# Output projections of a two-layer trunk kernel: tokens loaded two tiles of work ahead, the forms' loads on GpSimd's queue, the last pair of layer 0 in another order

## The chip, the cores and the metric

The kernel runs on one core of one Trainium2 chip. The metric is the device time of one execution in microseconds (us); the time of a kernel is the median of several runs. Engines are called as in the profile: PE is TensorE's matmul, PEld its weight load, DVE is VectorE, ACT ScalarE, POOL GpSimd, SP SyncE. A number such as L256 is line 256 of the kernel before unless the text says otherwise.

## The reference, cut to what matters

One inference step of a trunk with two layers, for 128 prompt tokens and 512 sample tokens (640 together), model width 2048. Everything is fp32.

```python
for layer in range(DEPTH):                       # DEPTH = 2
    hp = rms_norm(xp, norm_g[layer]) * (1.0 + sc_p) + sh_p      # prompt, 128 tokens
    hs = rms_norm(xs, norm_g[layer]) * (1.0 + sc_s) + sh_s      # sample, 512 tokens
    # even layer: banded attention and a gated short convolution
    # odd layer: differential attention and dense attention
    out_p, out_s = mixer(hp, ...), mixer(hs, ...)   # ends in:
    #   return jnp.concatenate([y_a, y_b], axis=-1) @ w_out
    xp = xp + gt_p * out_p                       # gated residual
    xs = xs + gt_s * out_s
```

The change touches the product with `w_out` (2048 x 2048) of both layers, and the `rms_norm` that follows the first layer's residual.

## The kernel before, in words

**Numbers in two parts.** Activations and weights lie transposed in SBUF, 128 channels by 640 tokens to a tile, 16 such tiles (`k` = 0 to 15) for the width. Each fp32 tile is split into a rounded part `hi` (ACT, L220) and the rest `lo` (DVE, L221); a product is three matmuls, weights hi by tokens hi, weights hi by tokens lo, weights lo by tokens hi (L256 to L258 in `proj_q`, L535 to L537 in `run_pairs`). A matmul moves 128 x 320, half of the tokens. A weight block of 512 x 128 is loaded as `raw` on SP's queue (L233) and split in the same way.

**An output projection** (`project_out`, `project`) makes 16 output tiles. The first three go together (`run_tiles`): for each quarter of the width in the order 0, 2, 1, 3 (a *unit*) the four token tiles of that quarter are split and used by the three output tiles, 72 matmuls in all. The fourth tile runs alone. The other 12 go in six pairs (`run_pairs`): seven products Q1, N5, P6, Q2, P7, Q3, P4 of 24 matmuls in place of eight. Four of these take halves of the tokens as they are, three take the *forms* T, sums and differences of halves that `forms` and `make_form` compute from the tiles `j` and `j + 8` (DVE L1083 to L1086 and the split, ACT the rounded part), eight forms in all; the fourth sum `d` goes to `room`, the first 1280 columns of `tables`.

**Where the tokens come from.** The mixers' results `y` are saved to DRAM (`yd`) on GpSimd's queue (L856) and come back twice: as `yin` for the split (SP's queue; layer 0 L865 for tiles 0 to 3 and L1127 for the rest, layer 1 L1586 for tiles 0 to 3 and 8 to 11 and L1127 for the rest) and as `w` for the forms (tag `w8`, four buffers, SP's queue, L1099). A queue takes its issues in the order of the program: a load that waits for a buffer holds back all that stands behind it. In `run_tiles` the four `yin` of a unit are asked for at the unit's start, behind the weights of that unit; L1127 takes the three buffers of `xr`.

**From layer 0 to layer 1.** The last pair's four results make halves of output tiles 14 and 15 (`x1_last`). Half 0 of the tokens is complete with P4's predecessor Q3, half 1 with P4. `norm_half` squares (L1262), sums over the channels with matmuls against ones (L1270: first the sum `acc` of the tiles before, then the last tile's `sq`), takes the power on POOL (L1275), spreads the result with matmuls against `ident` (L1281) and copies it to `sf` (ACT, L1284). Layer 1's first projection then makes its tokens `h` (DVE L1318, L1322, ACT L1320) half by half.

**PSUM.** A projection tile takes a pair of banks (pa, pb) with the number 0, 1 or 2 (`new_pp`; 2 is `Sp`); the three leading tiles take 0, 1, 2 in this order. The gate's result of the last mixer tile is read from its banks by L1003 and L1004.

Of the kernel before, what the change touches and what calls it, by code (L numbers as in the profile page):

```python
# [50 lines left out]
def trunk_kernel(ctx: ExitStack, tc: tile.TileContext, I: dict, O: dict):  # L51
# [195 lines left out]
    last_mm = [None]  # L247

    def proj_q(pp, part, qd, pos, halves=HV, alone=False, js=(0, 4)):
        wh, wl = part  # L250
        for half_i, sl in halves:
            ps = pp[half_i][:, 0:HALF]
            for j in range(*js):
                hi, lo = hs[qd * 4 + j]
                i = j - js[0]
                PE.matmul(ps, wh[:, i, :], hi[:, sl], start=(j == js[0] if alone else (pos == 0 and j == 0)), stop=False)  # L256
                PE.matmul(ps, wh[:, i, :], lo[:, sl], start=False, stop=False)  # L257
                last_mm[0] = PE.matmul(ps, wl[:, i, :], hi[:, sl], start=False,  # L258
                                       stop=(j == js[1] - 1 if alone else (pos == 3 and j == 3)))
# [57 lines left out]
    def run_tiles(jobs, w_ap, make_h, fill=None, rate=0.0, ahead=None, order=(0, 1, 2, 3), before=None,  # L317
                  last=None, by_half=False, mid=False, trans=[], grace=0, cut=None, summed=None, led=None, freed=None):
# [8 lines left out]
        else:  # L327
# [3 lines left out]
               else new_pp(1 + held.index(n) if trans else n) for n in leads}  # L331
# [112 lines left out]
    def run_pairs(cols, w_ap, mov, room, begin, out, tail):  # L444
# [47 lines left out]
        BANK = {"N5": "pb0", "Q3": "pb0", "Q2": "pb1"}  # L492
        seq = [(p, n) for p in range(len(cols)) for n in MOV]
# [32 lines left out]
        for i, (p, name) in enumerate(seq):  # L526
            bank, rows_, new = BANK.get(name, f"pa{(p + 1) % 2}"), mov[MOV[name]], name in ("Q1", "N5", "Q2")
# [22 lines left out]
            if name in ("Q2", "P7") and p == len(cols) - 1:  # L550
                tail(name)
# [306 lines left out]
    def y_maker(tags, width, held=()):  # L858
        def make(k):
            if k in held:  # L860
                drain(attn)
                t = y[k]
            else:
                t = pools["cur"].tile([P, width], F32, tag=tags[k % len(tags)], name="yin", bufs=4 // len(tags))[:, 0:NT]
                nc.sync.dma_start(t, ydram[k])  # L865
            hi, lo = new_h(k)
            split(hi, lo, t)
        return make


# [221 lines left out]
    def forms():  # L1092
# [3 lines left out]
        def load(j):  # L1096
            ts = [big("w8", bufs=4)[:, 0:NT] for _ in range(2)]
            for i in range(2):
                nc.sync.dma_start(ts[i], ydram[j + 8 * i])  # L1099
# [25 lines left out]
    def late_yin(k):  # L1125
        t = pools["cur"].tile([P, NT], F32, tag="xr", name="yin", bufs=3)
        nc.sync.dma_start(t, ydram[k])  # L1127
        split(*new_h(k), t)

# [7 lines left out]
    def project(w, cols, n0, maker, job, begin, out, tail, by_half=False):  # L1137

        go_on = run_tiles([(cols[n], job(n)) for n in range(3)], w, maker, order=(0, 2, 1, 3), by_half=by_half)


# [11 lines left out]
        for n in range(3, n0):  # L1153
            pp, t = new_pp((n - 3) % 2), 4 * (n - 3)
# [14 lines left out]
            if g is not None:  # L1169
# [5 lines left out]
                   "T2": form_of(0), "T3": form_of(1), "T4": form_of(2)}, room, begin, out, tail)  # L1175
        drain(prep)

    def project_out(l, maker, finish, last, tail):
# [35 lines left out]
        project(W_OUT[l], [n * P for n in range(KT)], n0, maker, job, begin, out, tail)  # L1214


    make_y0 = y_maker(("q0h", "q0l", "q1h", "q1l"), NT)
# [4 lines left out]
    def y0_maker(k):  # L1222
        if k < 4:
            return make_y0(k)
        if k == 8:
# [3 lines left out]
            st["acc"], st["sq"] = (mid_tile(n) for n in ("acc", "sq"))  # L1229
            attn.append(forms())  # L1230
        late_yin(k)
# [12 lines left out]
    def x1_last(t, h):  # L1244
        n, sl = KT - 2 + t, HV[h][1]
        if t != h:
            squares(n, sl)
            return
        nc.gpsimd.dma_start(xdram[n], st["xr", n])
        if h:  # L1250
            g = norm_half(n, h)
            advance([g], 1)
            advance([g], 1)
            drain(prep)
# [5 lines left out]
    def norm_half(n, h):  # L1260
        sl = HV[h][1]
        A.activation(st["sq"][:, sl], st["xr", n][:, sl], AF.Square)  # L1262
        yield
# [4 lines left out]
        for i, s in enumerate((st["acc"], st["sq"])):  # L1268
            for b, o in enumerate(starts):
                PE.matmul(tot[:, 4 * i + b:4 * i + b + 1], s[:, o:o + P], ones[:, 0:1], start=True, stop=True)  # L1270
            if i == 0:
                V.tensor_scalar(ss, tot[:, 0:3], 1.0 / D, EPS, ALU.mult, ALU.add)
            else:
                V.scalar_tensor_tensor(out=ss, in0=tot[:, 4:7], scalar=1.0 / D, in1=ss, op0=ALU.mult, op1=ALU.add)
        G.tensor_tensor(r, ss, half[:, 0:3], op=ALU.pow)  # L1275
        for _ in range(1 + h):
            yield
        rt = psT()
        with tc.issue_after(last_mm[0].ins) if h else ExitStack():
            for b, (o, w) in enumerate(((0, P), (P, P), (2 * P, HALF - 2 * P))):  # L1280
                PE.matmul(rt[:, o:o + w], r[:, b:b + 1].to_broadcast([P, P]), ident[:, P - w:P], start=True, stop=True)  # L1281
        if h == 0:
            st["rbc"] = big("sf")[:, 0:NT]
        A.copy(st["rbc"][:, sl], rt[:, 0:HALF])  # L1284
# [3 lines left out]
    def x1_tail(name):  # L1288

        if name == "Q2":  # L1290
            for k in range(4):
                x1_back(k, big("w8", bufs=4))
# [5 lines left out]
    project_out(0, y0_maker, x1_done, x1_last, x1_tail)  # L1298
# [276 lines left out]
    def y1_maker(k):  # L1575
        if k == 4:
# [5 lines left out]
        if k % 8 >= 4:  # L1582
            late_yin(k)
        else:
            t = pools["cur"].tile([P, 768], F32, tag="P", name="yin", bufs=P_BUFS)[:, 0:NT]
            nc.sync.dma_start(t, ydram[k])  # L1586
            split(*new_h(k), t)
# [32 lines left out]
    project_out(1, y1_maker, rows_out, rows_last, lambda name: None)  # L1620
# [49 lines left out]
```

## Time and profile before

| | us |
|---|---|
| median of 3 runs | 2295.93 (2293.33 to 2296.96) |
| the profiled execution, own time | 2294.4 |
| its span in the trace | 2292.6 |
| PE busy | 2255.9 (98%) |
| PEld busy | 2178.0 (95%) |
| DVE busy | 1589.8 (69%) |
| ACT busy | 1088.9 (47%) |
| POOL busy | 160.0 (7%) |

Places in the trace, counted from the span's start: layer 0's output projection begins at 915.5 us (first matmul of its first tile) and its pairs at 976.2; layer 1 begins at 1130.0, and layer 1's output projection at 2072.6.

How to read it: "busy" of PE adds up the modelled durations of pipelined matmuls, so that a PE at 98% can still lose time where no gap is seen; the number of matmuls in a window of fixed length shows it better. In a row of the timeline stand the start, the duration, engine, line, operation, what it writes and reads, and in brackets how long the engine sat idle before it and who released it. "SPq" and "POOLq" are the issues of DMAs by SP and POOL.

### The profile page before, as it was taken

Reading aid. Unit: us, or ns where it says so; the run is one execution under the profiler, and the core shown is the slowest. Engines: PE = TensorE matmul, PEld = TensorE weight load, DVE = VectorE, ACT = ScalarE, POOL = GpSimd, SP = SyncE. Lnnn points to the kernel's source line nnn. Section 1 sums busy time; section 2 is a strip of 40 time slices with the busy share of each in tenths; the row PEclk is TensorE's granted clock in tenths of the full one; section 3 lists DMA queues with packets and bytes.
Section 4 is the critical chain, followed back from the end, with each engine's and each line's share of the span. In section 5 each row is a group of like instructions: output and inputs, shape, how many; then the busy total and the mean of one; then the engine's idle time right before and its main releaser. Section 6 shows DMA issues by size and latency. Waiting matters only on the chain.

```text
span 2292.6 us, 41100 instructions
## 1 busy us (share of the span) xinstructions
PE 2255.9 (98%) x15900; PEld 2178.0 (95%) x15900; DVE 1589.8 (69%) x2831; ACT 1088.9 (47%) x2304; POOL 160.0 (7%) x224
## 2 busy tenths in 40 slices
PE   7999999999999999999999999999999999999999
PEld 5889999999999999999999999999999999999999
DVE  4666968779779776887787665365665655557775
ACT  5325652443522222544464443465565676755443
POOL 1001000000000000000100001011111100000101
PEclk9999999999999999999999999999999999999999
DMA  9985537547367564854553335223223221238642
GB/s 321 294 270 161 158 113 218 152 133 219 116 210 216 177 191 137 277 173 140 164 155 108 116 118 152 79 60 104 79 63 101 71 60 49 76 101 269 184 138 62
DMA packets 380899, 342.89 MB, mean 150 GB/s; under 512 B 16402, under 2 KB 338416, under 8 KB 380192
## 3 DMA queue, kind: packets, MB, share of 16 engines
q1 hardware_dynamic: 366288, 296.00, 43.0%
q0 software_dynamic: 13696, 42.10, 5.4%
q8 instruction: 125, 2.05, 0.4%
q10 hardware_dynamic: 720, 2.16, 0.3%
q14 instruction: 70, 0.57, 0.1%
HBM read 301.27 MB, written 38.93 MB: 148 GB/s over the span
## 4 chain that ended last, share of the span: by engine, by line
PE 85%; DVE 4%; ACT 4%; DMA 3%; issue 3%; POOL 1%; SPq 0%; ACTq 0%; POOLq 0%; DVEq 0%
PE pq L537 7%; PE pq L536 7%; PE pq L535 7%; PE pa L256 6%; PE pa L257 6%; PE pb L256 6%; PE pa L258 6%; PE pb L257 6%; PE pb L258 6%; PE pb L271 2%; PE pb L270 2%; PE pa L270 2%; PE pb L272 2%; PE pa L272 2%; PE pa L271 2%
## 5 line engine op out<-in xcount | busy, mean ns | idle before, releaser
L220 ACT ACTIVATE wh<-raw 128x512 fp32r<-128x512 f32 (+1 forms) x456 | 273.1, 600 | 574.0 <-PE pb L257 406.9
L221 DVE TENSOR_TENSOR wl<-raw,wh 128x512 fp32r<-128x512 f32 (+1 forms) x456 | 295.7, 650 | 212.3 <-ACT wh L220 191.9
L256 PE MATMUL pa<-h,wh 128*128 128x320 f32 x1024 | 325.3, 319 | 4.3 <-ACT h L220 2.0
L257 PE MATMUL pa<-h,wh 128*128 128x320 f32 x1024 | 319.5, 313 | 1.7 <-DVE h L221 0.8
L258 PE MATMUL pa<-h,wl 128*128 128x320 f32 x1024 | 318.2, 311 | 0.9 <-DVE wl L221 0.9
L257 PE MATMUL pb<-h,wh 128*128 128x320 f32 x1024 | 317.1, 310 | 0.0
L258 PE MATMUL pb<-h,wl 128*128 128x320 f32 x1024 | 316.8, 309 | 0.0
L256 PE MATMUL pb<-h,wh 128*128 128x320 f32 x1024 | 316.6, 310 | 0.0
L198 DVE SCALAR_TENSOR_TENSOR acc<-adaw,sT,acc 128x1024 f32<-128x1024 f32 x240 | 299.7, 1276 | 0.0
L256 PEld LDWEIGHTS pa<-h,wh 128*128 128x128 f32 x1024 | 193.1, 189 | 18.3 <-issue 10.0
L257 PEld LDWEIGHTS pa<-h,wh 128*128 128x128 f32 x1024 | 193.3, 189 | 7.6 <-issue 3.3
L535 PE MATMUL pq<-h,wh 128*128 128x320 f32 x640 | 198.7, 311 | 0.4 <-ACT wh L220 0.4
L537 PE MATMUL pq<-h,wl 128*128 128x320 f32 x640 | 198.0, 309 | 0.1
L536 PE MATMUL pq<-h,wh 128*128 128x320 f32 x640 | 197.7, 309 | 0.0
L258 PEld LDWEIGHTS pa<-h,wl 128*128 128x128 f32 x1024 | 193.1, 189 | 3.5 <-issue 2.1
L257 PEld LDWEIGHTS pb<-h,wh 128*128 128x128 f32 x1024 | 192.2, 188 | 1.0 <-issue 0.8
L256 PEld LDWEIGHTS pb<-h,wh 128*128 128x128 f32 x1024 | 192.1, 188 | 0.8 <-issue 0.4
L258 PEld LDWEIGHTS pb<-h,wl 128*128 128x128 f32 x1024 | 192.3, 188 | 0.0
L537 PE MATMUL pq<-T,wl 128*128 128x320 f32 x480 | 147.7, 308 | 0.2 <-DVE wl L221 0.2
L536 PE MATMUL pq<-T,wh 128*128 128x320 f32 x480 | 147.9, 308 | 0.0
L535 PE MATMUL pq<-T,wh 128*128 128x320 f32 x480 | 147.6, 308 | 0.1
L270 PE MATMUL pa<-h,wh 128*128 128x320 f32 x432 | 141.0, 326 | 0.0
(431 smaller groups left out, 5306.0 us busy)
## 6 DMA issues: line engine op xcount, KB each, us to landing
adaw<-in_ada_w SPq DMA_DIRECT2D x128, 512.0 KB, 4.3
raw<-in_ev_w_in SPq DMA_DIRECT2D x176, 256.0 KB, 3.5
raw<-in_od_w_in SPq DMA_DIRECT2D x160, 256.0 KB, 2.9
ada<-in_ada_w SPq DMA_DIRECT2D x32, 1024.0 KB, 7.9
w<-in_od_w_in SPq DMA_DIRECT2D x24, 512.0 KB, 4.0
yd<-y POOLq DMA_DIRECT2D x32, 320.0 KB, 3.2
yin<-yd SPq DMA_DIRECT2D x32, 320.0 KB, 4.5
w<-yd SPq DMA_DIRECT2D x32, 320.0 KB, 4.2
```

Of the source, the lines that this page charges most:

```text
L198: V.scalar_tensor_tensor(out=acc[c], in0=w, scalar=sT[:, kt, c:c + 1], in1=acc[c], op0=ALU.mult, op1=ALU.add)
L220: A.activation(hi, x, AF.Copy)
L221: V.tensor_sub(lo, x, hi)
L256: PE.matmul(ps, wh[:, i, :], hi[:, sl], start=(j == js[0] if alone else (pos == 0 and j == 0)), stop=False)
L257: PE.matmul(ps, wh[:, i, :], lo[:, sl], start=False, stop=False)
L258: last_mm[0] = PE.matmul(ps, wl[:, i, :], hi[:, sl], start=False, stop=(j == js[1] - 1 if alone else (pos == 3 and j == 3)))
L270: PE.matmul(ps, wh[:, j, :], hi[:, sl], start=(qd == 0 and j == 0), stop=False)
L271: PE.matmul(ps, wh[:, j, :], lo[:, sl], start=False, stop=False)
L272: PE.matmul(ps, wl[:, j, :], hi[:, sl], start=False, stop=(qd == 3 and j == 3))
L535: PE.matmul(ps, wh[:, j, :], hi, start=(new and h == 0 and j == 0), stop=False, **kw)
L536: PE.matmul(ps, wh[:, j, :], lo, start=False, stop=False, **kw)
L537: PE.matmul(ps, wl[:, j, :], hi, start=False, stop=(h == 1 and j == 3), **kw)
```

## The change

1. **Loads ahead.** `run_tiles` calls `ahead` for the next unit after the first tile of a unit. The output projections now hand it `y0_ahead` and `y1_ahead`, which issue the next unit's `yin`: in layer 0 tiles 8 and 9 go into the first 1280 columns of `tables`, 10 and 11 and then 4, 5, 6 and 12, 13, 14 into `xr`; 7 and 15 are still loaded at their split. In layer 1, 8 to 11 go to the buffers `P`, the rest to `xr`. The pool "even" is closed, and "mid" opened, at the call rather than at the split of tile 8.
2. **Forms' loads** are issued by GpSimd instead of SP.
3. **Banks** change places in layer 1's output projection (`flip`): the leading tiles take 1, 2, 0, and the pairs' banks are exchanged.
4. **The last pair of layer 0** runs Q1, N5, P6, P7, Q3, Q2, P4; its `xd` loads of layer 1's first tiles are issued at P7 and Q2 (two each) instead of all at Q2.
5. **The two norm halves** at the end of layer 0 are issued elsewhere. Half 1's matmuls are bound to follow particular matmuls of layer 1's first unit (`last_mm` holds four of them).

```diff
-                last_mm[0] = PE.matmul(ps, wl[:, i, :], hi[:, sl], start=False,
+                last_mm[j % 4] = PE.matmul(ps, wl[:, i, :], hi[:, sl], start=False,
...
-               else new_pp(1 + held.index(n) if trans else n) for n in leads}
+               else new_pp(1 + held.index(n) if trans else banks[n]) for n in leads}
...
-        BANK = {"N5": "pb0", "Q3": "pb0", "Q2": "pb1"}
-        seq = [(p, n) for p in range(len(cols)) for n in MOV]
+        LATE = ("Q1", "N5", "P6", "P7", "Q3", "Q2", "P4")
+        BANK = {"N5": f"pb{flip}", "Q3": f"pb{flip}", "Q2": f"pb{1 - flip}"}
+        seq = [(p, n) for p in range(len(cols)) for n in (LATE if late and p == len(cols) - 1 else MOV)]
...
             for i in range(2):
-                nc.sync.dma_start(ts[i], ydram[j + 8 * i])
+                nc.gpsimd.dma_start(ts[i], ydram[j + 8 * i])
...
+        go_on = run_tiles([(cols[n], job(n)) for n in range(3)], w, maker, order=(0, 2, 1, 3), by_half=by_half,
+                          ahead=ahead, banks=(1, 2, 0) if flip else (0, 1, 2))
...
+    def y0_ahead(qd, js):
+        if qd == 2:
             close("even")
             open_pool("mid")
             lay_out("T7 T6 T5 T4 sf xr w8 sx")
             st["acc"], st["sq"] = (mid_tile(n) for n in ("acc", "sq"))
+            for k in (8, 9):
+                yin_at(k, tables[:, (k - 8) * NT:(k - 7) * NT])
+        for k in range(4 * qd + (2 if qd == 2 else 0), 4 * qd + (4 if qd == 2 else 3)):
+            yin_load(k, "xr", 3)
+
+    def y0_maker(k):
+        yin_split(k, *(("q0h", "q0l", "q1h", "q1l")[k], 1) if k < 4 else ("xr", 3))
+        if k == 8:
             attn.append(forms())
...
     def norm_half(n, h):
         sl = HV[h][1]
         A.activation(st["sq"][:, sl], st["xr", n][:, sl], AF.Square)
-        yield
+        for _ in range(1 + h):
+            yield
+
+        def behind(j):
+            es = ExitStack()
+            if h:
+                es.enter_context(tc.high_priority())
+                es.enter_context(tc.issue_after(last_mm[j].ins))
+            return es
...
-        for _ in range(1 + h):
+        with behind(1):
...
+        if not h:
             yield
         rt = psT()
-        with tc.issue_after(last_mm[0].ins) if h else ExitStack():
+        with behind(3):
...
+    def y1_ahead(qd, js):
+        if qd == 2:
+            for k in range(8, 12):
+                yin_load(k, "P", P_BUFS, 768)
+            return
+        if qd == 1:
             drain(attn)
             close("odd")
             open_pool("fin")
             lay_out("T7 T6 xr T5 w8 sx sf T4")
             attn.append(forms())
+        for k in range(4 * qd, 4 * qd + 3):
+            yin_load(k, "xr", 3)
```

What this does to the order of the instructions is shown at three places. On SP, at layer 0's output projection, the issues stood like this from the last weights of the second unit on (`raw` is a weight block, `yin` a token tile for the split, `w8` a token tile for the forms; the number behind a name is the buffer's, `yd8` is the saved tile 8):

```order
L233 DMA raw_10813<-in_ev_w_out 128x4x128
L1127 DMA yin_10676<-yd8_160 128x640
L1127 DMA yin_10681<-yd9_161 128x640
L1127 DMA yin_10686<-yd10_162 128x640
L1099 DMA w8_10720<-yd0_152 128x640
L1099 DMA w8_10721<-yd8_160 128x640
L1127 DMA yin_10691<-yd11_163 128x640
L1099 DMA w8_10724<-yd1_153 128x640
L1099 DMA w8_10725<-yd9_161 128x640
L1127 DMA yin_10827<-yd4_156 128x640
L1099 DMA w8_10761<-yd2_154 128x640
```

Now SP's queue holds this from the same weights on (lines of the changed kernel; L863 is `yin_load`):

```order
L233 DMA raw_10817<-in_ev_w_out 128x4x128
L863 DMA yin_10612<-yd10_162 128x640
L863 DMA yin_10614<-yd11_163 128x640
L863 DMA yin_10735<-yd4_156 128x640
L233 DMA raw_10959<-in_ev_w_out 128x4x128
L863 DMA yin_10737<-yd5_157 128x640
L863 DMA yin_10739<-yd6_158 128x640
L233 DMA raw_10961<-in_ev_w_out 128x4x128
L863 DMA yin_10840<-yd7_159 128x640
```

The `w8` loads are gone from between the token tiles, and the third unit's weights stand four places behind the second's instead of sixteen. Tiles 8 and 9 are not in the piece: their two loads (L1219, into `tables`) stand far ahead on SP, beside the last weight loads before the tables' last reader. On POOL, the forms' loads now follow the last save of `y` and come before the first save of layer 0's result `xd`:

```order
L857 DMA yd15_167<-y_9817 128x640
L1098 DMA w8_10718<-yd0_152 128x640
L1098 DMA w8_10719<-yd8_160 128x640
L1098 DMA w8_10722<-yd1_153 128x640
L1098 DMA w8_10723<-yd9_161 128x640
L1098 DMA w8_10765<-yd2_154 128x640
L1098 DMA w8_10766<-yd10_162 128x640
```

In the kernel before, POOL's row for `yd15` was followed at once by the first save of `xd`; 16 loads have come between, and in layer 1 it is the same behind the save of `yd9`. On PE, at the end of layer 0, the last matmul of P4 was followed by half 1's `acc` sums, half 0's spread, half 1's `sq` sums, and then layer 1's first matmuls (`h_12933` is layer 1's first token tile):

```order
L537 MATMUL pq<-T_11054,wl 128x320
L1270 MATMUL T<-ones,acc 128x1 x3
L1281 MATMUL T<-ident,r_12852 128x128 x2
L1281 MATMUL T<-ident,r_12852 128x64
L1270 MATMUL T<-ones,sq 128x1 x3
L256 MATMUL pa<-h_12933,wh 128x320 x2
L256 MATMUL Sp<-h_12933,wh 128x320
L257 MATMUL pa<-h_12933,wh 128x320
```

Now half 0's sums and its spread stand in Q2, the last but one product; the piece is from Q2's last matmuls to P4's first:

```order
L1283 MATMUL T<-ones,sq 128x1 x3
L537 MATMUL pq<-h_10983,wh 128x320
L538 MATMUL pq<-h_10983,wl 128x320
L536 MATMUL pq<-h_10988,wh 128x320
L537 MATMUL pq<-h_10988,wh 128x320
L538 MATMUL pq<-h_10988,wl 128x320
L1294 MATMUL T<-ident,r_12816 128x128 x2
L1294 MATMUL T<-ident,r_12816 128x64
L536 MATMUL pq<-T_10728,wh 128x320
```

and half 1's stand among layer 1's first matmuls: its `acc` sums behind 15 of them, its `sq` sums 5 later, its spread 10 later (the piece is from the `sq` sums to behind the spread):

```order
L1283 MATMUL T<-ones,sq 128x1 x3
L256 MATMUL Sp<-h_12927,wh 128x320
L257 MATMUL pa<-h_12927,wh 128x320
L258 MATMUL pa<-h_12927,wl 128x320
L256 MATMUL pa<-h_12931,wh 128x320
L257 MATMUL pa<-h_12927,wh 128x320
L258 MATMUL pa<-h_12927,wl 128x320
L257 MATMUL pa<-h_12931,wh 128x320
L258 MATMUL pa<-h_12931,wl 128x320
L256 MATMUL pa<-h_12931,wh 128x320
L1294 MATMUL T<-ident,r_12949 128x128 x2
L1294 MATMUL T<-ident,r_12949 128x64
```

Behind this spread come seven more matmuls, and then the first one of the other half (`pb`). Between P4's last matmul and layer 1's first nothing stands any more.

109 lines of the change are left out of this document (46 added, 63 removed).

## The prediction

> **What bounds the kernel now.** I read the page first, then the waits of PE, then windows of equal kind laid side by side. The page's busy line, and three groups from the list of what PE waited for (us in total, times, longest):
>
> ```profile
> PE 2255.9 (98%) x15900; PEld 2178.0 (95%) x15900; DVE 1589.8 (69%) x2831; ACT 1088.9 (47%) x2304; POOL 160.0 (7%) x224
> ...
> PE pa L256 <- ACT h L220: 2.0, 3, 0.8
> PE pa L256 <- DVE gg L1004: 1.6, 1, 1.6
> ...
> PE T L1270 <- ACT sq L1262: 0.9, 1, 0.9
> ```
>
> TensorE is the bound, and a change can only pay where it removes a hole in PE. The holes near the change are small, and busy time hides part of them. So I count matmuls in windows; the columns are us, then the busy time of PE, PEld, DVE, ACT, POOL with the count, the granted clock, the DMA engines' share and GB/s:
>
> ```profile
> 1250.00:1300.00 50.00, 50.00 (x344) 50.00 (x343) 33.69 (x50) 22.07 (x42) 2.16 (x4) 1.00 0.39 116
> ...
> 920.00:927.00 7.00, 6.70 (x46) 6.43 (x44) 1.98 (x3) 2.02 (x3) 0.00 (x0) 1.00 0.82 265
> 927.00:957.00 30.00, 27.63 (x178) 26.24 (x179) 26.57 (x44) 16.64 (x24) 0.00 (x0) 1.00 0.90 290
> 957.00:988.00 31.00, 30.66 (x205) 29.68 (x204) 29.75 (x55) 16.32 (x29) 2.16 (x4) 1.00 0.90 278
> 1126.60:1139.30 12.70, 11.19 (x62) 10.60 (x61) 6.64 (x17) 4.81 (x11) 5.06 (x7) 0.73 1.09 366
> 2066.00:2082.00 16.00, 14.36 (x99) 14.09 (x98) 7.86 (x13) 5.17 (x9) 1.61 (x3) 1.00 0.65 213
> 2082.00:2112.00 30.00, 29.64 (x197) 28.55 (x196) 24.69 (x40) 16.12 (x23) 0.00 (x0) 1.00 0.89 293
> 2112.00:2142.00 30.00, 29.56 (x205) 28.99 (x205) 28.13 (x54) 16.57 (x32) 5.16 (x8) 1.00 0.92 279
> ```
>
> The first row is undisturbed: 50 / 344 = 0.1453 us a matmul. At that pace 920 to 988, the start of layer 0's output projection, would hold 468 matmuls and holds 46 + 178 + 205 = 429: 39 missing, **5.6 us**. 2066 to 2082 would hold 110 and holds 99: **1.6 us**; 2082 to 2142 would hold 413 and holds 402, **1.6 us**. At the border of the layers the window 1126.6 to 1139.3 holds 62, of which 24 are the small matmuls of L1270 and L1281. These are all the holes that the change can reach; the rest of the program is the same in order.
>
> **Part 1, layer 0's output projection.** SP's issues and PE's weight loads with their waits (start, duration, what, idle before, releaser):
>
> ```profile
> 900.93 19.93 SPq L233 DMA_DIRECT2D raw<-in_ev_w_out  x6
> 920.95 1.41 SPq L1127 DMA_DIRECT2D yin<-yd  x3
> 922.42 0.90 SPq L1099 DMA_DIRECT2D w<-yd  x2
> ...
> 937.71 1.52 SPq L233 DMA_DIRECT2D raw<-in_ev_w_out  x3
> ```
> ```profile
> 927.14 0.19 PEld L256 LDWEIGHTS pa<-h,wh 128*128 128x128 f32 x1 [0.71 <-ACT h L220]
> ...
> 942.29 0.19 PEld L256 LDWEIGHTS pa<-h,wh 128*128 128x128 f32 x1 [0.97 <-ACT h L220]
> ...
> 954.28 0.19 PEld L256 LDWEIGHTS pa<-h,wh 128*128 128x128 f32 x1 [1.09 <-ACT h L220]
> ...
> 984.81 0.19 PEld L537 LDWEIGHTS pq<-T,wl 128*128 128x128 f32 x1 [0.43 <-DVE wl L221]
> ```
>
> The weights' queue is full until 920.95, so the second unit's tokens are asked for 6 us before PE wants them; each later unit's tokens stand behind forms' loads that wait for a buffer. PE then waits for the split of a late tile, once in each of the three units. With the change tiles 8 and 9 are long in SBUF, the next ones are asked for a unit (72 x 0.1453 = 10.5 us) before their use, and no form's load stands in SP's way. The three waits should go. But DVE is the next limit: 26.57 of 30 and 29.75 of 31 us busy, and at the first pairs PE waits for it (the last row). PE can gain at the pairs only as much as DVE is ahead there. What the change brings DVE ahead: the `lo` parts of tiles 8 and 9 move into the time before 927, where DVE works 1.98 of 7 us, and one costs
>
> ```profile
> L221 DVE TENSOR_TENSOR h<-yin,h x32: 811/818/827, 902.7 to 2107.0; 128x640 fp32r<-128x640 f32 x32
> ```
>
> so 2 x 0.82 = 1.64 us leave the dense stretch. DVE's own idle time in 927 to 957 is 30 - 26.57 = 3.43 us. It comes from late tiles and late forms' loads as well as from waits for ACT, and I choose half of it, 1.7 us, as recoverable. **Term 1: -(1.64 + 1.7) = -3.3 us**; ends: -1.6 if only the two moved splits count, -5.6 if all missing matmuls come back. It costs nothing to issue the forms' loads on POOL as long as POOL is free: the row
>
> ```profile
> 918.50 0.54 POOL L856 DMA_DIRECT2D yd<-y  x1 [57.54 <-DVE y L1006]
> ```
>
> is its last of `y` and comes after 57.54 us of nothing; what stands behind the 16 loads there, layer 0's first save of `xd`, is needed only at the next layer. That POOL takes these loads no faster than DVE frees the four buffers is the order that SP had too.
>
> The Trainium skill, "DMA: Bandwidth & Descriptors", section "Rules for kernel authors", speaks against this part: spreading DMAs over SP, ACT and GpSimd does not help bandwidth, since all of them run on the same 16 engines and interleave; it saves only the issue time of a sequencer. The windows agree as far as they go: the engines are at 0.82 to 0.92 already. By that rule only what changes in the order of issue can pay, and rival B is what it would make of the time.
>
> **Part 2, the border of the layers.** DVE's and POOL's rows of half 0 and half 1, PE's rows, and one window:
>
> ```profile
> 1121.99 0.49 DVE L1206 TENSOR_TENSOR tables<-pq,tables 128x320 f32<-128x320 f32 x1
> ```
> ```profile
> 1126.24 0.88 POOL L1275 TENSOR_TENSOR r<-ss,half 128x3 f32<-128x3 f32 x1 [1.70 <-DVE ss L1274]
> ...
> 1130.44 1.10 POOL L1275 TENSOR_TENSOR r<-ss,half 128x3 f32<-128x3 f32 x1 [2.06 <-DVE ss L1274]
> ```
> ```profile
> 1126.63 0.72 PE L1270 MATMUL T<-ones,acc 128*128 128x1 f32 x6
> 1127.21 0.86 PE L1281 MATMUL T<-ident,r 128*128 128x128 f32 x6
> 1128.96 1.19 PE L1270 MATMUL T<-ones,sq 128*128 128x1 f32 x6 [0.88 <-ACT sq L1262]
> 1130.01 0.88 PE L256 MATMUL pa<-h,wh 128*128 128x320 f32 x2
> ...
> 1136.76 0.78 PE L1281 MATMUL T<-ident,r 128*128 128x128 f32 x6
> ...
> 1139.33 0.52 PE L256 MATMUL pb<-h,wh 128*128 128x320 f32 x2
> ```
> ```profile
> 1132.00:1134.00 2.00, 2.00 (x8) 2.00 (x9) 1.37 (x4) 0.56 (x1) 1.97 (x3) 0.50 1.01 396
> ```
>
> From 1126.63 to 1139.33 pass 12.7 us. In them are four groups of small matmuls, 1127.21 - 1126.63 = 0.58 us each at full speed, 2.3 us, and 62 - 24 - 2 = 36 large ones (the two of P4 at the window's left edge taken off), 5.2 us. The other **5.2 us** are lost: gaps, and 8 matmuls in 2 us instead of 14 at a granted clock of 0.50.
>
> Now the same chains in the new order. Half 0: from the start of Q3's last sum (1121.99) to the power's end (1126.24 + 0.88 = 1127.12) are 5.1 us; one more sum of DVE (`acc`, of the kind of the first row, a net 0.4) now stands in this chain: 5.5. Behind Q3 PE now has Q2, 24 x 0.1453 = 3.5 us, with two groups of sums, 1.2 us, before the spread: 4.7. PE waits 0.8. From the spread to the first `h` before (1127.21 to 1130.01) were 2.8 us; P4's 3.5 us cover it, no wait. Half 1: P4's end to the `sq` sums took 1128.96 - 1126.63 = 2.3 us; now 20 matmuls and the `acc` sums, 3.5 us, stand between, no wait. `sq` sums to the power's end took 1131.54 - 1128.96 = 2.6 us; now 0.58 + 10 x 0.1453 = 2.0, a wait of 0.5. Spread to the first `pb` took 1139.33 - 1136.76 = 2.6 us; now 0.58 + 7 x 0.1453 = 1.6, a wait of 1.0. Together 2.3 of 5.2 stay lost: **term 2, -2.9 us**; ends: -1.0 (DVE, with layer 1's tokens to make at the same time, delays each step) and -4.7 (only one wait of 0.5 stays).
>
> The clock: PE was nearly idle from 1126.63 to 1130.01 and then ran at 0.50, in 1132 to 1134 still. The 1.6 us hole before layer 1's output projection left it at 1.00. I count no half clock, since no hole in the new order is over 1.0 us. The Trainium skill, "TensorE: Matmul & The Clock Gate", Part 1, has the clock halved after an idle window of about 3.4 us that runs freely; the trace agrees, with 3.4 us of low activity, and by that rule too the new order keeps the full clock.
>
> **Part 3, layer 1's output projection.** PE's first row there, then the save of tile 9, its load, its split, and the waits in the second unit:
>
> ```profile
> 2072.57 0.42 PE L256 MATMUL pa<-h,wh 128*128 128x320 f32 x1 [1.64 <-DVE gg L1004]
> ```
> ```profile
> 2075.40 0.54 POOL L856 DMA_DIRECT2D yd<-yl  x1 [2.65 <-DVE yl L1006]
> ...
> 2078.86 1.29 SPq L1586 DMA_DIRECT2D yin<-yd  x3
> ...
> 2082.03 2.37 ACT L220 ACTIVATE h<-yin 128x640 fp32r<-128x640 f32 x3 [1.63 <-DMA yin<-yd]
> ```
> ```profile
> 2084.53 0.19 PEld L257 LDWEIGHTS pa<-h,wh 128*128 128x128 f32 x1 [0.37 <-DVE h L221]
> 2085.32 0.19 PEld L257 LDWEIGHTS pa<-h,wh 128*128 128x128 f32 x1 [0.34 <-DVE h L221]
> ```
>
> The first tile wants the banks that the last gate is still being read from. With the banks exchanged PE begins 1.6 us sooner. But that is lent, not won: tile 9 is made by that same last gate, is saved at 2075.40, and can be loaded only when the save has landed, near 2078.8, whatever stands on SP. Its split, and those of 10 and 11 behind it, end when they ended before, and PE already waited for two of them. So the 1.6 us come back in the second unit, as a longer wait for `h`. Worse, the forms' second pair (tiles 1 and 9) is now asked for at the same moment on POOL's queue, 0.66 MB beside the 0.98 MB of tiles 9 to 11; at the 293 GB/s of this stretch that is up to 2.2 us more for the last, nothing if it comes late. I take 0.7, a third. What remains to be won are the 1.6 us missing in 2082 to 2142 less the two waits above (0.7): 0.9, for the third and fourth units' tiles, now asked for a unit ahead, and for the forms, whose loads no longer stand behind raw weights at 2083 to 2094. **Term 3: -0.9 + 0.7 = -0.2 us**; ends -1.6 (no meeting of loads, and half of the bank's hole won) and +1.4 (2.2 - 0.8).
>
> **The sum.** -3.3 - 2.9 - 0.2 = -6.4 us. The profiled execution took 2294.4 us (its span 2292.6 and 1.8 around it): 2288.0. The median of the runs, 2295.93, is 1.5 above that execution, so the forecast is **2289.5 us**. Its own ends: the small gains, -1.6 - 1.0 + 1.4 = -1.2, give 2294.7, all large ones, -5.6 - 4.7 - 1.6 = -11.9, give 2284.0.
>
> **Rivals.**
> A. *Forecast*, chance 0.65.
> B. *DVE, or the DMA engines, give layer 0's advance back.* The start of layer 0's output projection is dense on DVE (29.75 of 31) and on the DMA engines (0.90); what is asked for earlier only lands beside the forms' tiles, and PE waits at the pairs for what it did not wait for before. For it: both shares. Against it: DVE's idle 3.43 us and the 5 idle ones of 920 to 927. Then term 1 is nothing: 2295.9 - 2.9 - 0.2 = **2292.8**, chance 0.15.
> C. *Slower: forms' loads ahead of the tokens.* On a queue of their own the forms' loads start at once and as a pair move 2 x 0.328 = 0.66 MB, at the 265 GB/s of 920 to 927 2.5 us of all engines. If each of the three later units in both layers had its last tile late by that, 6 x 2.5 = 15.0 us come and terms 1 and 3 go: 2295.9 - 2.9 + 15.0 = **2308**. It decides where a tile takes longer than the 10.5 us it is asked for ahead, less two splits of 0.82. The page's list of DMA issues has medians (last column, us) of
>
> ```profile
> yin<-yd SPq DMA_DIRECT2D x32, 320.0 KB, 4.5
> w<-yd SPq DMA_DIRECT2D x32, 320.0 KB, 4.2
> ```
>
> so they would have to double. Tiles 7 and 15 have no such lead, though. Chance 0.12.
> D. *It does not do what it says:* the tiles stand ahead in the queue but wait for buffers as before, and the norm's chain stays as long as it was. **2294 to 2297**, chance 0.08.
>
> **How the numbers follow.** The likeliest is A, 2289.5. The range of 8 in 10 is 2283 to 2296: it holds A and B and about half of D. This kernel's measurement can tell about 0.2%, 4.6 us, from no change, so "faster" is below 2291.3, where A's own ends lie on both sides. A gives 0.55 of its 0.65 to "faster" and B 0.03: 0.58. "Same" takes A's 0.10, B's 0.12 and D's 0.06: 0.28. "Slower" is C and the rest of D: 0.14.
>
> **What would show it right or wrong.** Right: in 68 us from 4.5 us behind the first matmul of layer 0's output projection the count rises from 429 to about 450; no wait for `h` above 0.5 us there; the granted clock stays 1.00 through the border, where PE waits near 0.8, 0.5 and 1.0 us; no wait for `gg` at layer 1's output projection, and one of 1.5 to 3 us for `h` in its second unit. Wrong: landing times of `yin` near 9 us in every unit (C); PE waiting for `wl` or `T` at the first pairs for as long as it waited for `h` (B); a clock of 0.50 at the border again.

## The result, and the profile after

The changed kernel takes **2311.28 us** (median of 6 runs, 2309.05 to 2314.49), the kernel before 2296.44 (6 runs): a ratio of 1.0067, 95% interval 1.0054 to 1.0079. It is 15 us **slower**; the forecast was 2289.5, 6.4 us faster than the median it started from. The profiled execution's span is 2308.9 us, 16.3 longer than the one of before.

The page's busy line and its list of DMA issues (last column: median us from issue to landing):

```profile
PE 2259.5 (98%) x15900; PEld 2180.8 (94%) x15900; DVE 1588.2 (69%) x2831; ACT 1086.0 (47%) x2304; POOL 177.0 (8%) x256
...
w<-yd POOLq DMA_DIRECT2D x32, 320.0 KB, 5.0
yin<-yd SPq DMA_DIRECT2D x30, 320.0 KB, 4.9
```

PE is busy 3.6 us longer with the same 15900 instructions, so most of the 16 us are holes. Both kinds of load take longer than before (4.2 and 4.5). What PE waited for (us in total, times, longest):

```profile
PE pa L256 <- ACT h L220: 5.8, 2, 4.4
...
PE pa L257 <- DVE h L221: 3.3, 5, 1.6
...
PE T L565 <- ACT ot L1607: 2.2, 1, 2.2
PE Sp L256 <- ACT wh L220: 2.0, 1, 2.0
```

The wait for the gate's banks (`gg`) is gone, as meant. In its place one wait of 4.4 us stands for the split of a token tile.

**Where the time went** is found most sharply by numbering the large matmuls (128 x 320) of PE: both kernels have 12,576, and up to a few at the border of the layers the n-th of one is the n-th of the other. The n-th's start in one trace less its start in the other, taken at stage marks, gives each stage's loss. Worked out so from the trace's rows of PE (us against the profiled execution of before; the times are those of before):

```
                        changed   before, again   forms on SP
to 913 (other code)       +1.5        +1.2           +3.9
913-992  output proj. 0   +4.2        +1.1           -0.8
992-1118 pairs            +0.2         0.0           +0.2
1118-1145 border          -2.7        +0.3           -2.7
1145-1214 layer 1 begins  +2.6        -0.3            0.0
1214-2073                 -2.1        -1.1           -1.6
2073-2087 output proj. 1  +6.9        +0.1           +0.7
2087-2144                 +5.8        +0.8           +1.6
2144-end                   0.0         0.0            0.0
sum                      +16.3        +2.2           +1.1
```

The second column is a second execution of the unchanged kernel: it shows what two executions differ by, most of it ahead of 913 us and between 1214 and 2073. The third column is an experiment below.

**The two output projections.** Layer 0, SP's and POOL's issues, ACT's split of the tokens, PE's weight loads:

```profile
891.82 30.49 SPq L233 DMA_DIRECT2D raw<-in_ev_w_out  x9
922.41 1.77 SPq L863 DMA_DIRECT2D yin<-yd  x3
```
```profile
920.59 2.16 POOL L1098 DMA_DIRECT2D w<-yd  x4
```
```profile
929.14 2.36 ACT L220 ACTIVATE h<-yin 128x640 fp32r<-128x640 f32 x3 [4.42 <-DMA yin<-yd]
```
```profile
929.92 0.19 PEld L256 LDWEIGHTS pa<-h,wh 128*128 128x128 f32 x1 [1.59 <-ACT h L220]
930.78 0.19 PEld L257 LDWEIGHTS pa<-h,wh 128*128 128x128 f32 x1 [0.67 <-DVE h L221]
...
968.32 0.19 PEld L256 LDWEIGHTS pa<-h,wh 128*128 128x128 f32 x1 [1.22 <-ACT wh L220]
```

On SP nine weight blocks stand ahead of the tokens, each waiting for a buffer. In the kernel before there were nine as well, over the same 30.49 us (the prediction's row of six begins only at 900):

```profile
890.37 30.49 SPq L233 DMA_DIRECT2D raw<-in_ev_w_out  x9
```

So tiles 10, 11 and 4 are asked for at 922.41, no sooner than tiles 8 to 10 were before (920.95, and this kernel is 1.5 us late by then). 1.8 us ahead of them POOL has asked for four forms' tiles, 1.3 MB. Tile 10 can be split at 929.14, 6.7 us after its issue, and PE waits for it. Then, in the single tile (968), PE waits for weights whose split on ACT stands behind late forms.

Layer 1, the same engines:

```profile
2080.48 0.54 POOL L857 DMA_DIRECT2D yd<-yl  x1 [1.57 <-DVE yl L1005]
2081.01 1.65 POOL L1098 DMA_DIRECT2D w<-yd  x3
2084.32 0.54 POOL L1098 DMA_DIRECT2D w<-yd  x1 [1.65 <-DMA yd<-yl]
```
```profile
2083.81 2.21 SPq L863 DMA_DIRECT2D yin<-yd  x3
```
```profile
2090.98 2.35 ACT L220 ACTIVATE h<-yin 128x640 fp32r<-128x640 f32 x3 [7.07 <-DMA yin<-yd]
```
```profile
2091.76 0.29 PEld L256 LDWEIGHTS pa<-h,wh 128*128 128x128 f32 x1 [4.69 <-ACT h L220]
```

Tile 9 is asked for at 2083.81, when its save has landed, and arrives 7.2 us later; before, the same step took 2082.03 - 2078.86 = 3.2. Three windows around it (columns as in the prediction):

```profile
2081.00:2086.00 5.00, 5.00 (x36) 5.00 (x35) 0.80 (x2) 0.63 (x1) 2.17 (x5) 1.00 0.98 277
2086.00:2091.00 5.00, 1.34 (x10) 1.07 (x8) 0.00 (x0) 0.02 (x1) 0.00 (x0) 1.00 0.99 371
2091.80:2097.80 6.00, 5.78 (x20) 5.35 (x21) 2.98 (x4) 1.97 (x3) 0.00 (x0) 0.50 0.51 182
```

In the second window PE, DVE and ACT stand still while the DMA engines are full (0.99), so it isn't that nothing was moved, but that the wrong thing was moved first. Full engines alone don't make tile 9 late: in the kernel before they stood at 0.97 from 2080 to 2085, and it arrived after 3.2 us. And after the hole PE runs 6 us at half the granted clock: 20 matmuls where 41 would fit, 3.1 us more. The trace has three stretches at 0.50, 13.7 us together; before, there was one of 6.8.

**The border** went as the prediction had it. PE's weight loads with a wait:

```profile
1129.70 0.74 PEld L1294 LDWEIGHTS T<-ident,r 128*128 128x128 f32 x6 [0.64 <-POOL r L1288]
...
1139.84 0.74 PEld L1294 LDWEIGHTS T<-ident,r 128*128 128x128 f32 x6 [0.28 <-POOL r L1288]
1142.47 0.30 PEld L256 LDWEIGHTS pb<-h,wh 128*128 128x128 f32 x2 [0.94 <-ACT h L1332]
1150.81 0.19 PEld L256 LDWEIGHTS Sp<-h,wh 128*128 128x128 f32 x1 [2.22 <-ACT wh L220]
```

The chain's three waits are 0.64, 0.28 and 0.94 (0.8, 0.5 and 1.0 were forecast). The row at 1150.81 is new: layer 1's weights, queued on SP behind ten tiles that cannot be loaded before P4, are late for a PE that arrives sooner. It took 2.6 us back in this execution.

### The profile page after: what moved, and what is told of

Read it like the earlier page. It is cut to its first block, busy times and chain, and to the rows that moved or that the text cites. A ratio compares the mean times of both kernels' runs of the same rounds, so it can differ in the third digit from the quotient of the medians.

```text
span 2308.9 us, 41111 instructions
## 1 busy us (share of the span) xinstructions
PE 2259.5 (98%) x15900; PEld 2180.8 (94%) x15900; DVE 1588.2 (69%) x2831; ACT 1086.0 (47%) x2304; POOL 177.0 (8%) x256
## 4 chain that ended last, share of the span: by engine, by line
PE 69%; issue 20%; DVE 4%; ACT 3%; DMA 3%; POOL 1%; POOLq 0%; DVEq 0%; ACTq 0%; SPq 0%
PE pq L538 7%; PE pq L537 7%; PE pq L536 7%; PE pa L256 4%; PE pa L257 4%; PE pa L258 4%; PE pb L256 3%; PE pb L257 3%; PE pb L258 3%; PE pb L271 2%; PE pb L270 2%; PE pb L272 2%; PE pa L270 2%; PE pa L272 2%; PE pa L271 2%
```

## The experiments

Theory **T**: two queues share the DMA engines, so a transfer on POOL's queue delays what SP asks for; the forms' loads are there at the moment at which the second unit's tokens are asked for, and the tokens, the forms behind them on DVE and PE's clock all pay. Rivals: **R1**, the earlier token loads hold back weights; **R2**, the border; **S**, POOL's loads are slow in themselves, whatever they meet; **F**, it is the forms' loads as such and not the traffic. Eleven runs follow.

### Forms' loads back on SP

```diff
-                nc.gpsimd.dma_start(ts[i], ydram[j + 8 * i])
+                nc.sync.dma_start(ts[i], ydram[j + 8 * i])
```

> The changed kernel with the forms' loads back on SP's queue; all else as changed. Theory T (the forms' loads, free on POOL's queue, are first at the DMA engines and make the token tiles of the second unit late; matched matmul by matmul the changed kernel lost 4.4 us at layer 0's output projection and about 11 at layer 1's): both losses go, 2311.3 - 15.4 = 2296, or a few us less if the earlier token loads win something, so 2292 to 2297. Rival R1 (the earlier token loads hold back the weights behind them): 2305 to 2312. Rival R2 (the reworked border of the layers is the loss): about as the changed kernel, 2308 to 2312.

Measured: 2294.72 us against 2296.93 of before, ratio 0.9987 (0.9979 to 0.9996). One line of code is worth 16.6 us, and without it the change is a small gain. SP, ACT and PE at the same place in layer 1:

```profile
2078.11 1.29 SPq L863 DMA_DIRECT2D yin<-yd  x3
2079.93 0.38 SPq L233 DMA_DIRECT2D raw<-in_od_w_out  x1
2080.36 1.45 SPq L863 DMA_DIRECT2D yin<-yd  x3
2081.85 1.92 SPq L1098 DMA_DIRECT2D w<-yd  x4
```
```profile
2080.99 1.60 ACT L220 ACTIVATE h<-yin 128x640 fp32r<-128x640 f32 x2 [1.81 <-DMA yin<-yd]
```
```profile
2083.50 0.19 PEld L257 LDWEIGHTS pa<-h,wh 128*128 128x128 f32 x1 [0.41 <-DVE h L221]
```

On one queue the transfers come in the order of their issue: tile 9 after 2.9 us, the forms' tiles after the tokens. The stage 2073 to 2087 loses 0.7 us instead of 6.9. R1 and R2 fall.

### Only the forms' loads on POOL

The kernel before, with the line of the diff above as the change has it (`nc.gpsimd`).

> The kernel before with the forms' loads on GpSimd's queue and nothing else changed. Theory T: the token tiles are asked for later still than in the changed kernel, and the forms' loads meet them: slower by 5 to 15 us, 2301 to 2311. Rival R1 and R2: nothing of their causes is in it, 2294 to 2299.

Measured: 2308.61 us, ratio 1.0052 (1.0040 to 1.0064). By stages: +4.5 us from 913 to 992, +6.1 from 2073 to 2087, +6.2 from 2087 to 2144. This edit alone costs 11.7 of the 15 us, in the three stages in which the changed kernel loses most; R1 and R2 have no part in it.

### Only the border, and only the earlier token loads

The kernel before with parts 4 and 5 of the change (order of the last pair, norm halves, `xd` loads) and nothing else:

```diff
+        LATE = ("Q1", "N5", "P6", "P7", "Q3", "Q2", "P4")
...
+        with behind(1):
```

> The kernel before with only the last pair in the order Q1, N5, P6, P7, Q3, Q2, P4, the norm halves issued elsewhere, and layer 1's first tiles loaded at P7 and Q2. Theory T: the chain wins 2.8 us as in the changed kernel, and the weights of layer 1, queued behind its tiles, take 3.7 back (with a stretch at half clock): 2295 to 2299. The prediction's own term 2: 2296.4 - 2.9 = 2293.5. Rival R2: 2302 or more.

Measured: 2296.18 us, ratio 0.9996 (0.9987 to 1.0004). The stage of the border gains 2.7 us here, and between 2.70 and 2.75 in all other kernels with this part but the one with the tokens on POOL (1.7). In the stage behind it 0.2 us come back here, 2.6 in the changed kernel, up to 3.6 in others: whether the late weights cost anything differs from execution to execution. The median doesn't show the gain clear of its interval, since executions differ by up to 4 us ahead of 913 us.

The kernel before with part 1 (`y0_ahead`, `y1_ahead`, the tables' place) and nothing else:

```diff
+            for k in (8, 9):
+                yin_at(k, tables[:, (k - 8) * NT:(k - 7) * NT])
```

> The kernel before with only the earlier token loads (8 and 9 in the tables' place), forms' loads on SP. Theory T: these are not the loss; they win 1 to 4 us at layer 0, nothing at layer 1: 2292 to 2296. Rival R1: 2303 or more.

Measured: 2297.32 us, ratio 0.9999 (0.9991 to 1.0008). From 913 to 992 it gains 1.1 us against the first execution of before (2.1 against the second). It doesn't lose, as R1 has it. The stage gains about the least that was forecast, and the time, above the forecast's 2296, doesn't show it: the profiled execution is 4.3 us late by 913 already, and loses 3.6 from 2087 to 2144.

### Forms' loads held back until the tokens are there

```diff
+                if j < 2:
+                    A.activation(ts[i][:, 0:1], hs[11][0][:, 0:1], AF.Copy)
                 nc.gpsimd.dma_start(ts[i], ydram[j + 8 * i])
```

> The changed kernel with the forms' loads on POOL's queue as changed, but the first four of them held back until tile 11 of the second unit has arrived (each buffer's first column is written by ACT from the split tile 11 before the load; the load overwrites it). Theory T (two queues share the DMA engines, so that 1.3 MB of forms' loads make the tokens late): the wait of 4.7 us for tokens in layer 1's second unit falls to under 1 us, layer 0's of 1.6 to under 0.5, and no stretch at half clock follows; the forms now start some 6 us later than in the kernel before, which may cost up to 3 us at the pairs: 2297 to 2304. Rival S (loads on POOL's queue are slow in themselves, or DVE holds them up, whatever they meet): landing times stay at 5 us in the median and the loss stays, 2307 to 2314.

Measured: 2309.25 us, ratio 1.0051 (1.0037 to 1.0065). ACT and POOL in layer 1:

```profile
2087.69 1.54 ACT L220 ACTIVATE h<-yin 128x640 fp32r<-128x640 f32 x2 [2.27 <-DMA yin<-yd]
```
```profile
2091.12 2.21 POOL L1100 DMA_DIRECT2D w<-yd  x4 [9.37 <-ACT w L1099]
```

Tile 9, asked for at 2084.70, arrives after 3.0 us, and the stage 2073 to 2087 loses 0.7 us, as with forms on SP; layer 0's second unit gains 1.0 where the changed kernel lost 1.6. The page's list of DMA issues:

```profile
w<-yd POOLq DMA_DIRECT2D x32, 320.0 KB, 4.6
yin<-yd SPq DMA_DIRECT2D x30, 320.0 KB, 4.2
```

The tokens are back at 4.2 (4.9 in the changed kernel). So the first part of T is shown: what delays the tokens is what is asked for beside them. But the time was forecast too low by 5 us and lies where S had put it: the loss has moved, not gone, +7.7 us from 931 to 992 and +5.9 from 2087 to 2144. In layer 0 the forms do begin late (the first is done 23.0 us behind the first matmul of the output projection, with forms on SP 17.7), and the clock fell to 0.50 twice there (from 969.3 for 6.8 us and from 986.3 for 3.4), which T had excluded. In layer 1 they don't begin late. DVE's last step for the first and for the eighth form there (the split into `T`), in this kernel, then in the one with forms on SP:

```profile
2099.82 1.16 DVE L221 TENSOR_TENSOR T<-sx,T 128x960 fp32r<-128x960 f32 x1
2144.36 1.16 DVE L221 TENSOR_TENSOR T<-sx,T 128x960 fp32r<-128x960 f32 x1
```
```profile
2094.78 1.16 DVE L221 TENSOR_TENSOR T<-sx,T 128x960 fp32r<-128x960 f32 x1 [1.12 <-ACT T L220]
2134.23 1.15 DVE L221 TENSOR_TENSOR T<-sx,T 128x960 fp32r<-128x960 f32 x1
```

Counted from the first matmul of layer 1's output projection (2077.7 and 2071.5), the first form is done after 23.3 us here and after 24.5 with forms on SP. But the eighth follows 44.5 us behind the first here, and 39.4 there. That is the second way in which the changed kernel pays: its forms follow one another more slowly (44.8). In all traces, 42.1 to 44.8 us pass from a layer's first form to its eighth where POOL loads them (seven layers), and 37.7 to 41.1 where SP does (nineteen). Their loads behind the first four take 4.4 to 5.2 us in the mean on POOL and 3.6 to 4.4 on SP, and POOL issues them 0.3 us after their buffer is free, SP mostly 0.03.

### The two queues exchanged

```diff
-        nc.sync.dma_start(yin[k], ydram[k])
+        (nc.gpsimd if k >= 4 else nc.sync).dma_start(yin[k], ydram[k])
...
-                nc.gpsimd.dma_start(ts[i], ydram[j + 8 * i])
+                nc.sync.dma_start(ts[i], ydram[j + 8 * i])
```

> The changed kernel with the two queues exchanged: the token tiles from 4 on are loaded by POOL, the forms' tiles and the weights by SP. Theory T: a queue of their own puts the tokens first and the forms behind the weights: waits for tokens in the second units under 0.5 us, 2292 to 2299. Rival S (POOL's loads are slow in themselves): the tokens land after 6 us and more, PE waits for them in every unit, 2302 or more.

Measured: 2303.45 us, ratio 1.0027 (1.0017 to 1.0037). The time is in S's range and not in T's as I had put it; the rows show which of the two is wrong, and where. Issues of POOL and SP, and ACT's splits of tiles 9, 10 and 11:

```profile
2079.57 0.54 POOL L863 DMA_DIRECT2D yin<-yd  x1 [2.92 <-PE Sp L258]
2081.29 2.71 POOL L863 DMA_DIRECT2D yin<-yd  x5 [1.18 <-issue]
```
```profile
2080.87 1.93 SPq L1098 DMA_DIRECT2D w<-yd  x4
```
```profile
2082.71 0.74 ACT L220 ACTIVATE h<-yin 128x640 fp32r<-128x640 f32 x1 [3.01 <-DMA yin<-yd]
2086.60 0.74 ACT L220 ACTIVATE h<-yin 128x640 fp32r<-128x640 f32 x1 [3.15 <-DMA yin<-yd]
2088.12 0.74 ACT L220 ACTIVATE h<-yin 128x640 fp32r<-128x640 f32 x1 [0.79 <-DMA yin<-yd]
```

The first tile on POOL's queue, asked for 1.3 us before SP's first forms' load, is there 3.1 us after its issue: POOL's queue alone does not make a token late by several us, as S needs. (The smaller difference between the forms' loads on the two queues is not excluded by this.) The next, issued while SP's four forms' loads run, takes 5.3. A queue of its own does not put the tokens first; it only makes them share. The stage 2073 to 2087 loses 6.8 us, layer 0's nearly nothing (0.4).

### Traffic that nobody needs

The kernel with forms on SP, with four extra loads on POOL:

```diff
+            for k in range(4):
+                t = pools["cur"].tile([P, 5, P], F32, tag="ot", name="extra", bufs=2)
+                nc.gpsimd.dma_start(t.rearrange("p a b -> p (a b)"), ydram[k])
             attn.append(forms())
```

> The kernel with the forms' loads on SP (all else as changed), plus four loads of 320 KB on POOL's queue behind the last save of layer 1, into buffers that are not yet in use, two at a time; nothing reads them. Theory T (any transfer that runs on a second queue at that moment makes the tokens late): tiles 9 to 11 land 1 to 4 us later than without, PE waits that much longer in the second unit of layer 1, and everything behind moves by it: 2296 to 2302, with the loss between the first matmul of layer 1's output projection and the 96th behind it. Rival F (it is the forms' loads themselves, their place in POOL's program or their buffers, and not the traffic): 2292 to 2296, as with forms on SP.

Measured: 2297.1 us, ratio 0.9999 (0.9990 to 1.0008), against 0.9987 without the extra loads. POOL, SP and ACT:

```profile
2076.19 1.13 POOL L1599 DMA_DIRECT2D extra<-yd  x2 [1.48 <-DMA yd<-y]
```
```profile
2076.99 1.29 SPq L863 DMA_DIRECT2D yin<-yd  x3
```
```profile
2081.34 0.74 ACT L220 ACTIVATE h<-yin 128x640 fp32r<-128x640 f32 x1 [3.81 <-DMA yin<-yd]
```

Tile 9 takes 4.4 us instead of 2.9, and the stage 2073 to 2087 loses 3.8 instead of 0.7. Loads that no form uses make the tokens late too, so F is not needed for the second unit.

### Layer 0 alone, no exchange of banks, tile 9 in place

POOL's queue for the forms of layer 0 only:

```diff
-            attn.append(forms())
+            attn.append(forms(nc.gpsimd))
...
-            attn.append(forms())
+            attn.append(forms(nc.sync))
```

> The changed kernel with the forms' loads on POOL's queue in layer 0 alone, on SP in layer 1. Theory T, by the matched matmuls: the loss of layer 0, about 5 us against forms on SP, and what the border gives back with it, 2.5: 2298 to 2303. If the loss were one of layer 1 alone, 2293 to 2297.

Measured: 2302.89 us, ratio 1.0022 (1.0012 to 1.0031): +3.0 us from 913 to 992, and 3.6 given back behind the border. By the medians layer 0's forms on POOL cost 8.2 us over forms on SP, and layer 1's the other 8.4 of the changed kernel: about half each, though the part behind the border differs from execution to execution.

Forms on SP, without part 3:

```diff
-                late=l == 0, flip=l)
+                late=l == 0, flip=0)
```

> The changed kernel with the forms' loads on SP and without the exchange of banks in layer 1. By the traces so far the exchange gains 1.2 to 1.6 us at the first matmul of layer 1's output projection and gives back at least 0.7 in the second unit, since tile 9 is saved no sooner: within 1 us of the kernel with forms on SP, 2293 to 2297. If the exchange wins what it frees (the prediction's upper end), 2296 to 2298.

Measured: 2295.4 us, ratio 0.9989 (0.9980 to 0.9997), against 0.9987 with the exchange. It makes no difference that can be seen. By stages, kernels with it gain 1.6 to 2.1 us from 1214 up to the first matmul of layer 1's output projection where those without it gain 0.4 to 1.2; with forms on SP 0.7 is lost right behind.

Forms on SP, and tile 9 of layer 1 split from where the gate left it:

```diff
-            for k in range(8, 12):
+            for k in (8, 10, 11):
                 yin_load(k, "P", P_BUFS, 768)
+            yin[9] = y[9]
```

> The kernel with the forms' loads on SP (all else as changed), and tile 9 of layer 1 split from where the gate left it in SBUF instead of from its copy in DRAM, so that the second unit no longer waits for the save. If the save of tile 9 is what takes the exchanged banks' gain back, the wait in layer 1's second unit goes (0.6 to 1.5 us less than with forms on SP): 2292.5 to 2294.5. If it is the loads of 10 and 11 or DVE: as with forms on SP, 2294 to 2296.

Measured: 2293.29 us, ratio 0.9982 (0.9974 to 0.9991), the fastest kernel here. The same 15 us at the start of layer 1's output projection, first in the kernel with forms on SP, then in this one:

```profile
2073.00:2088.00 15.00, 14.40 (x94) 13.58 (x93) 6.83 (x11) 4.95 (x8) 0.54 (x1) 1.00 0.87 307
```
```profile
2072.00:2087.00 15.00, 15.00 (x105) 15.00 (x104) 9.85 (x17) 6.36 (x10) 0.54 (x1) 1.00 0.83 288
```

PE has no hole left (105 matmuls for 103 at the undisturbed pace). The wait for the save of tile 9, which held back the loads of 10 and 11 behind it as well, was what took the exchanged banks' gain back. The stage 2073 to 2087 gains 0.8 us where forms on SP lost 0.7; the medians of these two kernels are too close to tell them apart.

### The kernel before, again

> The kernel before once more, to see by how much its stages differ between two profiled executions: up to 4 us in the first 240 us and up to 3 in the stage from 2087 to 2144, where kernels with no change there differed by 1.4 to 3.6; under 0.5 us in the stages of layer 0's output projection.

Measured: 2296.57 us; the stages are in the table above. They differ by 1.1 us from 913 to 992, more than I had said, by 1.1 from 1214 to 2073, and by 0.8 from 2087 to 2144. So single stages of a profile are read to about 1 us, and losses of 4 to 7 are clear of that.

## Why the prediction was wrong, point by point

- **The bound** was read rightly: PE, and holes of a few us in the three places that were named.
- **Term 1** (-3.3): wrong in sign in the changed kernel, +4.2. The step that failed is the sentence "It costs nothing to issue the forms' loads on POOL as long as POOL is free". POOL's time was not the price. The price is paid on the DMA engines, first by the tiles on the other queue (1.6 us at tile 10), then by the forms, which follow one another more slowly. The edit of that sentence alone, in the kernel before, costs 11.7 us, 4.5 of them in this stage. With forms on SP the term is -0.8 (-1.9 against the second execution of before): the right sign, at the small end. A second step failed with it: the tokens are not asked for a unit, 10.5 us, ahead. SP's queue has the same nine weight blocks ahead of them as before and issues tile 10 at 922.41, 5.9 us before PE wants it. And with forms on SP the forms' loads stand between the token tiles again, so that kernel does not show what the term would be with both cured.
- **Term 2** (-2.9): right, -2.7 in the changed kernel and in seven others, with its three waits near their forecast size and no half clock inside. What was missing is what comes next: layer 1's weights stand behind ten tile loads that wait for P4, and a PE that is 2.7 us sooner meets them (2.2 us in the changed kernel).
- **Term 3** (-0.2): wrong by some 12 us. "The 1.6 us come back in the second unit" held with forms on SP as far as one can see (0.7 of them), and the tile in place supports the reason given for it. The meeting of loads was named, and sized at 0.7 with 2.2 as its end. It cost 6.9 - 0.7 = 6.2 in the second unit, of which some 3 are the half clock behind the hole. The sizing divided one pair's bytes by the rate. In fact three forms' loads stood ahead of the tokens and a fourth beside them, and tile 9 took 4.0 us longer than before. And the price did not end there: from 2087 to 2144 the changed kernel lost 5.8 us, the six profiles with all of these loads on SP and nothing extra 0.8 to 3.6, in the mean 2.0. The forms' own loads take 5.0 us in place of 4.4 in the median, and from the first form of layer 1 to the eighth pass 44.8 us in place of 39.4; the sum had no term for that.
- **The rivals.** Rival C was the one that came true: "forms' loads ahead of the tokens", with 2308 for a price and a chance of 0.12. Its mechanism is shown, its place only in part: it named the three later units of both layers, and the waits stand in the second unit and among the forms. That its size was about met is partly luck, since the slower forms and the half clock were not in it. Its argument against itself failed: "It decides where a tile takes longer than the 10.5 us it is asked for ahead" supposed the same lead that term 1 did. B, with no loss but the gain's, is not what happened, though DVE did stand still for tokens (4.06 us at 929.90).
- **The signs** named for a wrong forecast were the useful part, in kind more than in size: landings of `yin` grew to 7.7 us at most and 4.9 in the median, not to 9 in every unit; PE waited for `wl` in layer 0's single tile; and the clock fell to 0.50, not at the border but 7 us behind it and in layer 1's output projection. The count of matmuls in 68 us of layer 0's output projection was to rise to 450; it fell from 427 to 401 (429 was the sum of three windows, which counts two at the edges twice), and with forms on SP it rose to 432.

The Trainium skill, "DMA: Bandwidth & Descriptors", section "Queues, rings and completion order", says that each DMA engine takes turns between the queue rows that have work for it, a packet at a time. The runs agree as far as the order goes: in every trace the loads of one queue landed in the order of their issue throughout both output projections, but in the changed kernel the forms' load issued on POOL at 2084.32, 0.5 us after tile 9, landed 0.2 us before it. Tile 9 took 2.9 us with forms on SP, and 4.4 to 7.2 beside loads issued earlier on a second queue. I had quoted the same page's rule that more queues bring no bandwidth, and had drawn from it only that the gain might vanish, not that the order of arrival is given up.

**Left open.** Why the forms follow one another more slowly is shown only as far as their longer loads go: whether a load on POOL takes longer because of the queue itself or because of what runs beside it was not told apart, nor how much of the 5.8 us from 2087 to 2144 this is. A late first form by itself is not the price there: with the queues exchanged, and forms on SP, it is done 29.4 us behind the first matmul, as in the changed kernel (29.1), and that stage loses 2.5 us. Why the weights behind the border cost something in some executions (1.6, 2.6 and 3.6 us) and not in others (0.0 to 0.5) wasn't tried.

## What to carry to other kernels

A queue is also a priority: here loads that shared one arrived in the order in which they were issued, and moving the less urgent ones to a second queue let them overtake. Before a load is moved, list what else is in flight at that moment and what each of them delays, and don't count the issuing engine's time alone. And ask of each "loaded ahead" at which time its issue really comes, behind what stands in its queue.

## What was not expected of the hardware

- With the DMA engines at a share of 0.98 to 0.99, transfers on a second queue went with a landing of 7.2 us for a 320 KB tile that took 2.9 to 3.2 on one queue; the engines moved 277 and 371 GB/s in the two windows, 323 in the kernel before from 2080 to 2085.
- One hole of 4.7 us in PE was followed by 6 us at a granted clock of 0.50, 20 matmuls for 41. The Trainium skill, "TensorE: Matmul & The Clock Gate", Part 1, has the clock halved after an idle window of about 3.4 us. The trace agrees for this hole; two other stretches of 3.4 us at 0.50 (from 1152.3 and from 2145.6) follow holes of only 2.2 and 2.4 us, and here the measurement goes beyond the page. The hole's length alone does not decide: one of 2.4 us that ends at 238.26 left the clock at 1.00.
